# Hyena mixer, last MLP and grouped-query mixer of a diffusion trunk rebuilt, GpSimdE's element-wise work on VectorE

## The chip, the cores and the metric

One core of a Trainium2 chip runs the whole program in one launch. The metric is the device time of one execution in microseconds (us), the median of several runs. The engines are TensorE (PE; PEld is its weight load), VectorE (DVE), ScalarE (ACT), GpSimdE (POOL) and SyncE (SP), which issues the DMAs.

## What is computed

One step of a transformer-like trunk of four layers on 640 tokens (128 of context, 512 latent ones on a grid of 64 columns) of width 1024, all in float32. Each layer is a mixer and a squared-ReLU MLP of hidden width 4096, with modulation ahead of each and a gated, normalised residual after each. The mixers are differential attention, neighbourhood attention, grouped-query attention and a Hyena convolution. The parts that the change touches, shortened:

```python
def centred_short_conv(u, w, b):
    up = jnp.pad(u, ((0, 0), (1, 1), (0, 0)))
    return up[:, :L] * w[0] + up[:, 1:L + 1] * w[1] + up[:, 2:L + 2] * w[2] + b

def long_conv(z, freq_resp):
    zf = jnp.fft.rfft(z, n=2 * L, axis=1)
    return jnp.fft.irfft(zf * freq_resp[None], n=2 * L, axis=1)[:, :L]

def hyena(h, ...):
    parts = jnp.split(centred_short_conv(h @ w_in, short_w, short_b), 3, axis=-1)
    z = parts[0]
    for o in range(2):
        z = parts[o + 1] * (long_conv(z, freq_resp[:, o]) + z * filter_bias[o])
    return z @ w_o

# grouped-query attention: q and k are RMS-normalised per head, scaled, turned by the axial rotary
# every sublayer: x = layer_norm(ALPHA * x + gate * sublayer(modulate(x, shift, scale)), g, b)
# MLP: square(relu(h @ w1)) @ w2
```

## The kernel before

Every float32 product runs as three TensorE products of split operands: a high part and a low part of each side (`mm3`, lines 473 to 475). So each operand is split once: ScalarE rounds the high part and VectorE subtracts to get the low part (`w_convert` for weights, lines 450 and 451; `ln_out` for the activations `hh` and `hl`, lines 740 and 742; `k_stack` and similar helpers in the attention mixers). In `ln_out` the subtraction of the latent half for three of the five token tiles stands on GpSimdE.

A sublayer ends with its output product in quarters of 256 columns. `residual` multiplies each by the gate on VectorE (line 653) and adds it to the running sum `r` (line 660) on VectorE or GpSimdE, by a counter. Then the statistics of the norm are taken per token tile (line 689) and the next sublayer's input is formed. The norm's own scale and shift of `r` (`ln_tile`, lines 748 and 749, four 512-column steps per tile) follow behind.

The filters of the Hyena layer are made during earlier layers (`hy_filter` work, lines 1600 to 1624): a 512-column product, a window, a sum on VectorE and a difference on GpSimdE (line 1619, the "taps"), and a store to `ab_d`.

The third mixer projects both key pairs first, takes the reciprocal root of their mean squares, and, in `tail`, spreads that factor by TensorE (`rk`), turns the key with the rotary tables, whose swapped copy `sw` comes by DMAs from the other partitions, scales it, and stacks high and low parts of the key pair and of the cached key (`k_stack`). The query heads then follow in a stream of units, of which the first for context keys begins with the product `sc` (line 2203) of `qc`.

The Hyena mixer works in four groups of 256 channels and two orders, so eight times: the input is transposed and split (`zt`), multiplied by a DFT matrix in two halves of the frequencies (`kt`), and for each half VectorE forms sums and differences of the spectrum (line 1771), four 256-column products `pi` (line 1779; three of them on GpSimdE), one 1024-column product `pr` (1780), the combinations (1781 to 1784), ScalarE and VectorE split the result into `yy` (1785, 1788), and TensorE multiplies it back (`py`, 1798 and 1801). `feed` puts products of the next group's input projection (`hyin`) in between. One room, `hywork`, holds the intermediate values of both halves. The short convolution (`hy_conv`, line 1713) is a chain of fused steps on rows that are interleaved in pairs.

Within an MLP, chunks of four hidden tiles are closed by products with `w2` in quarters of 256 columns and collected in `sums` (line 882).

TensorE's order of work is mostly set by a tile scheduler from the order of the code; the waits follow from it.

## Time and profile before

| | |
|---|---|
| Time, median of 3 runs (lowest, highest) | 3380.49 us (3379.76, 3384.22) |
| Profiled execution | 3378.87 us, span 3376.8 us |
| Mean granted TensorE clock | 0.993 |
| Busy: TensorE, VectorE, ScalarE, GpSimdE | 97%, 71%, 46%, 11% |
| GpSimdE, us and instructions | 385.7 us, 476 |

The span is the time from the first to the last instruction in the trace; the execution's time adds what lies around it. A share of busy time is a mean over stages with different limits, so that 97% says how much TensorE could give back at most and not where. Starts in the rows below are in us from the beginning of the span.

### The profile page before, as it was taken

Reading aid. Unit: us, or ns where it says so; the run is one execution under the profiler, and the core shown is the slowest. Engines: PE = TensorE matmul, PEld = TensorE weight load, DVE = VectorE, ACT = ScalarE, POOL = GpSimd, SP = SyncE. Lnnn points to the kernel's source line nnn. Section 1 sums busy time; section 2 is a strip of 40 time slices with the busy share of each in tenths; the row PEclk is TensorE's granted clock in tenths of the full one; section 3 lists DMA queues with packets and bytes.
Section 4 is the critical chain, followed back from the end, with each engine's and each line's share of the span. In section 5 each row is a group of like instructions: output and inputs, shape, how many; then the busy total and the mean of one; then the engine's idle time right before and its main releaser. Section 6 shows DMA issues by size and latency. Waiting matters only on the chain.

```text
span 3376.8 us, 63034 instructions
## 1 busy us (share of the span) xinstructions
PE 3278.9 (97%) x25288; PEld 3162.6 (94%) x25288; DVE 2396.6 (71%) x4682; ACT 1552.0 (46%) x2832; POOL 385.7 (11%) x476
## 2 busy tenths in 40 slices
PE   8999999999999999999998999999999999999998
PEld 6888999998999899999997889999998999999998
DVE  4777877877765685777678878667769888723347
ACT  3667654333455654334345655433334334432322
POOL 0000101111322310000121020000021112100002
PEclk9999999999999999999999999999999999999999
DMA  8454245554343325556321123555523233222321
GB/s 287 143 158 129 65 149 177 174 189 150 102 139 101 120 83 187 169 188 214 118 72 48 36 66 105 173 177 181 185 68 127 84 114 134 96 76 76 101 76 51
DMA packets 162757, 429.40 MB, mean 127 GB/s; under 512 B 20574, under 2 KB 30438, under 8 KB 159390
## 3 DMA queue, kind: packets, MB, share of 16 engines
q1 hardware_dynamic: 162464, 425.37, 39.0%
q8 instruction: 199, 3.26, 0.4%
q14 instruction: 94, 0.77, 0.1%
HBM read 371.20 MB, written 34.05 MB: 120 GB/s over the span
## 4 chain that ended last, share of the span: by engine, by line
PE 78%; DVE 10%; issue 4%; ACT 3%; DMA 2%; POOL 2%; SPq 0%; DVEq 0%; POOLq 0%; ACTq 0%
PE w L473 18%; PE w L474 17%; PE w L475 17%; PE qk L473 3%; PE qk L474 2%; PE qk L475 2%; PE s L2038 2%; PE ptp L1088 2%; PE pv L2085 2%; PE pv L2189 1%; PE v L475 1%; PE py L1801 1%; PE v L474 1%; PE v L473 1%; DVE hl L451 1%
## 5 line engine op out<-in xcount | busy, mean ns | idle before, releaser
L451 DVE TENSOR_TENSOR hl<-raw,hl 128x1024 fp32r<-128x1024 f32 x411 | 515.9, 1256 | 395.4 <-ACT hl L450 378.2
L474 PE MATMUL w<-hl,ff 128*128 128x256 f32 x2560 | 714.2, 279 | 0.0
L475 PE MATMUL w<-hl,ff 128*128 128x256 f32 x2560 | 713.7, 279 | 0.0
L473 PE MATMUL w<-hl,ff 128*128 128x256 f32 x2560 | 713.6, 279 | 0.0
L450 ACT CAST hl<-raw 128x1024 fp32r<-128x1024 f32 x411 | 430.1, 1047 | 573.5 <-PE w L475 477.9
L473 PE MATMUL w<-hh,hl 128*128 128x320 f32 (+2 forms) x2048 | 637.0, 311 | 7.2 <-ACT fx L894 6.7
L474 PE MATMUL w<-hl,hl 128*128 128x320 f32 (+2 forms) x2048 | 633.3, 309 | 3.3 <-DVE hl L742 3.3
L475 PE MATMUL w<-hh,hl 128*128 128x320 f32 (+2 forms) x2048 | 633.2, 309 | 0.0
L474 PEld LDWEIGHTS w<-hl,ff 128*128 128x128 f32 x2560 | 480.7, 188 | 1.7
L473 PEld LDWEIGHTS w<-hl,ff 128*128 128x128 f32 x2560 | 480.4, 188 | 1.7
L475 PEld LDWEIGHTS w<-hl,ff 128*128 128x128 f32 x2560 | 479.6, 187 | 0.0
L541 DVE SCALAR_TENSOR_TENSOR ada<-adaw,sil,ada 128x512 f32<-128x512 f32 x504 | 358.0, 747 | 95.4 <-DMA adaw<-in_ada_w 92.6
L473 PEld LDWEIGHTS w<-hh,hl 128*128 128x128 f32 x2048 | 385.1, 188 | 23.1 <-ACT fx L894 9.5
L474 PEld LDWEIGHTS w<-hl,hl 128*128 128x128 f32 x2048 | 385.1, 188 | 4.1 <-DVE hl L742 4.1
L475 PEld LDWEIGHTS w<-hh,hl 128*128 128x128 f32 x2048 | 385.3, 188 | 0.0
L894 ACT ACTIVATE fx<-w 128x640 f32<-128x640 f32 (+2 forms) x136 | 91.5, 672 | 465.0 <-PE w L475 448.3
L882 DVE TENSOR_TENSOR sums<-sums,w 128x256 f32<-128x256 f32 x400 | 164.1, 415 | 128.4 <-PE w L475 127.9
L473 PE MATMUL qk<-hh,hl 128*128 128x320 f32 (+2 forms) x672 | 214.5, 319 | 0.2
L474 PE MATMUL qk<-hl,hl 128*128 128x320 f32 (+2 forms) x672 | 210.9, 314 | 1.7 <-DVE hl L742 1.7
L660 POOL TENSOR_TENSOR r<-r,gtmp 128x256 f32<-128x256 f32 x146 | 120.7, 834 | 782.6 <-DVE gtmp L653 739.6
L475 PE MATMUL qk<-hh,hl 128*128 128x320 f32 (+2 forms) x672 | 209.3, 311 | 0.0
L473 PE MATMUL w<-hl,oh 128*128 128x256 f32 x640 | 184.0, 288 | 7.6 <-DVE gtmp L653 5.4
(342 smaller groups left out, 6734.9 us busy)
## 6 DMA issues: line engine op xcount, KB each, us to landing
raw<-in_w SPq DMA_DIRECT2D x256, 512.0 KB
adaw<-in_ada_w SPq DMA_DIRECT2D x288, 256.0 KB
adaw<-in_ada_w SPq DMA_DIRECT2D x16, 1024.0 KB
raw<-ab_d SPq DMA_DIRECT2D x32, 512.0 KB
raw<-in_hy_in SPq DMA_DIRECT2D x24, 512.0 KB
ks<-ks SPq DMA_DIRECT2D x64, 160.0 KB
adaw<-in_ada_s SPq DMA_DIRECT2D x8, 1024.0 KB
raw<-in_da_qk SPq DMA_DIRECT2D x16, 512.0 KB
```

Source lines behind the costliest of these rows:

```text
L450: self.nc.scalar.copy(t[:, 0], raw)
L451: self.nc.vector.tensor_sub(t[:, 1], raw, t[:, 0].bitcast(F32))
L473: mm(ps, w[0], x[0], start=start, stop=False)
L474: mm(ps, w[0], x[1], start=False, stop=False)
L475: mm(ps, w[1], x[0], start=False, stop=stop)
L541: nc.vector.scalar_tensor_tensor(out=y, in0=raw[h], scalar=x, in1=y, op0=ALU.mult, op1=ALU.add)
L660: eng.tensor_add(rv, rv, tmp)
L882: nc.vector.tensor_add(v, v, ps)
L894: nc.scalar.activation(x, src, AF.Relu)
L1088: nc.tensor.transpose(ps[:, i * P:(i + 1) * P], pr[:, (done + i) * P:(done + i + 1) * P], self.ident)
L2038: mm(ps[dst], hd["qs"][h][:, self.qs], ks[:, c], start=n == 0, stop=n == 1)
L2085: nc.tensor.matmul(ps[64 * h:64 * h + 64], self.v[:, self.chunk + c, vc:vc + 64], pts[h][:, c * P:(c + 1) * P], start=c == 0, stop=c == se ...
```

## The change

- All residual adds, all subtractions of `ln_out`, the taps, the rotary products, and the low parts of `k_stack` in the third mixer are on VectorE. The scaling of the context units' output (line 2218, two mixers) goes from GpSimdE to two ScalarE steps. GpSimdE keeps the neighbourhood bias, the last norm and zeroing.
- Third mixer: of the norm of `r` left over from the MLP ahead, three of five tiles are taken during the keys' projection and two after the first key pair is stacked. One reciprocal root serves both key pairs; only the first pair is turned, scaled and stacked ahead of the query stream, the second in steps within it.
- Hyena: both halves' spectra are formed ahead of the first half's filtering, in rooms of their own; the `pi` products are two 512-column steps. The short convolution works on rows with eight columns of padding, on 512 columns at a time.
- Last MLP: chunks 0 to 5 are closed with products of 512 columns, 720 for 1440, with `w2` packed for it.

The core of the diff:

```diff
@@ residual
-        eng = nc.vector if quick or self.scale_r or self.rt < self.share else nc.gpsimd
...
-            eng.tensor_add(rv, rv, tmp)
+            nc.vector.tensor_add(rv, rv, tmp)
@@ ln_out
-            sub = nc.gpsimd.tensor_sub if h == 0 and t in (0, 2, 3) else nc.vector.tensor_sub
-            self.last_dve = sub(self.hl[:, f, c], x, self.hh[:, f, c].bitcast(F32))
+            self.last_dve = nc.vector.tensor_sub(self.hl[:, f, c], x, self.hh[:, f, c].bitcast(F32))
@@ mlp
+        def wide_close(ch):
+            for h in range(2):
+                pss = [self.any1([P, 512], "w2") for _ in range(NT - 1)]
+                if h == 0:
+                    two = self.b2([P, 2, 512], "w2")
+                pss.append(two[:, h])
+                for kp in range(2):
+                    u = self.wget(("w2", l, 4 * ch + 2 * h + kp))
+                    for t, ps in enumerate(pss):
+                        c = slice(t * P, (t + 1) * P)
+                        for k in range(2):
+                            f = slice(k * 512, (k + 1) * 512)
+                            self.mm3(ps, (ff[ch][:, 0, 2 * kp + k, c], ff[ch][:, 1, 2 * kp + k, c]), (u[:, 0, f], u[:, 1, f]), kp + k == 0, kp + k == 2)
+                        if kp:
+                            collect(ps, t, h * 512, ch == 0)
...
+            if last and ch < 7:
+                wide_close(ch - 1)
+                continue
@@ third mixer
             for i, x in enumerate(xk):
...
+                for t in ((NT - 1, 0), (1,))[i]:
+                    with self.tc.issue_after(self.last_dve.ins):
+                        self.ln_tile(t)
+            next(values)
+            next(values)
+            for i in range(2):
+                sums(sqs[i], list(factors(i))[1])
+            self.rsqrt(*factors(None), 1.0 / 64)
+            wides = [spread(0)]
+            turn_key(0, xk[0])
+            next(values)
+            next(values)
+            scale_key(0, xk[0], wides[0])
+            self.man.close()
+            for h in range(2):
+                stack_key(0, xk[0], h)
+            later = [lambda: turn_key(1, xk[1]), lambda: scale_key(1, xk[1], spread(1)), lambda: stack_key(1, xk[1], 0), lambda: stack_key(1, xk[1], 1)]
+            with self.tc.issue_after(self.stacked.ins):
+                for t in (2, 3):
+                    self.ln_tile(t)
@@ filter taps
-            nc.gpsimd.tensor_sub(v[:, 256:512], win[:, 0:256], win[:, 256:512])
+            nc.vector.tensor_sub(v[:, 256:512], win[:, 0:256], win[:, 256:512])
@@ hy_conv
-        acc(xl[:, 0, 1:], ul[:, 1, 0:n], w0)
-        acc(xl[:, 0, 0, 1:], ul[:, 1, n, 0:r], w0)
-        acc(xl[:, 1], ul[:, 0], w0)
-        acc(xl[:, 0], ul[:, 1], w2)
-        acc(xl[:, 1, 0:n], ul[:, 0, 1:], w2)
-        acc(xl[:, 1, n, 0:r], ul[:, 0, 0, 1:], w2)
+        acc(y, u[:, base - ROWS:end - ROWS], w0)
+        for e in range(2):
+            acc(xl[:, e], pairs(u[:, base + ROWS:end + ROWS])[:, e], w2, pairs(y)[:, e])
@@ hy_order
-            for q in range(2):
-                for s in range(2):
-                    eng = nc.vector if q * s else nc.gpsimd
-                    eng.tensor_mul(pi[:, q, s], z4[:, q, s], h4[:, q, 1 - s])
+        def filtered(kt):
+            z4, h4 = zs[kt], hs[:, kt]
+            for s in range(2):
+                nc.vector.tensor_mul(pi[:, :, s], z4[:, :, s], h4[:, :, 1 - s])
             nc.vector.tensor_mul(pr, z4, h4)
...
+        for kt in range(2):
+            spectrum(kt)
+        filtered(0)
+        feed(FB)
+        back(0)
+        filtered(1)
+        feed(FC)
+        back(1)
```

Three places show how the order moves. The first is VectorE in one Hyena order, from the products of the first half on (`hywork` the shared room, `hs` the filter's spectrum, `zf` the forward product). Before:

```order
L1771 TENSOR_TENSOR hywork<-zf_30730,hywork 128x512 x2
L1779 TENSOR_TENSOR hywork<-hywork,hs_30647 128x256
L1780 TENSOR_TENSOR hywork<-hywork,hs_30647 128x1024
L1782 TENSOR_TENSOR hywork<-hywork 128x2x256
L1781 TENSOR_TENSOR hywork<-hywork 128x2x256
L1784 TENSOR_TENSOR hywork<-hywork 128x512 x2
L1713 SCALAR_TENSOR_TENSOR x_30796<-u_30553,hsw,x_30796 128x127
L1788 TENSOR_TENSOR yy_30729<-hywork,yy_30729 128x512 x2
```

and now:

```order
L1846 TENSOR_TENSOR hywork<-zf_30752,hywork 128x512 x2
L1851 TENSOR_TENSOR hywork<-hywork,hs_30666 128x2x256 x2
L1852 TENSOR_TENSOR hywork<-hywork,hs_30666 128x1024
L1853 TENSOR_TENSOR hywork<-hywork 128x2x256
L1854 TENSOR_TENSOR hywork<-hywork 128x2x256
L1846 TENSOR_TENSOR hywork<-zf_30780,hywork 128x512 x2
L1856 TENSOR_TENSOR hywork<-hywork 128x512 x2
L1778 SCALAR_TENSOR_TENSOR x_30846<-u_30572,hsw,x_30846 128x127
L1778 SCALAR_TENSOR_TENSOR cv_30851<-u_30572,hsw,cv_30851 128x512
```

The four `pi` products, of which only one stood here (the other three are on GpSimdE), are two VectorE steps, and the second half's sums (line 1846 with another `zf`) stand ahead of the first half's output. The second place is VectorE at the third mixer's start, around the key's factors (`ss` the sums of squares, `r` the residual in its norm). Before, after eighteen of the norm's twenty steps:

```order
L749 TENSOR_TENSOR r_13383<-r_13383,ln_b_18377 128x512
L749 TENSOR_TENSOR r_13383<-r_13383,ln_b_18381 128x512
L1405 COPY misc_20120<-ss_20381 128x10
L1405 COPY misc_20120<-ss_20438 128x10
L1170 TENSOR_SCALAR misc_20120<-misc_20120 128x10
L451 TENSOR_TENSOR hl_20577<-raw_20134,hl_20577 128x1024
L1171 TENSOR_SCALAR misc_20120<-misc_20120 128x10
```

and now, after ten of the twelve that stand there:

```order
L752 TENSOR_TENSOR r_13390<-r_13390,ln_b_18385 128x512
L752 TENSOR_TENSOR r_13390<-r_13390,ln_b_18389 128x512
L457 TENSOR_TENSOR hl_20538<-raw_20142,hl_20538 128x1024
L1430 COPY misc_20128<-ss_20410 128x10
L1430 COPY misc_20128<-ss_20417 128x10
L1195 TENSOR_SCALAR misc_20128<-misc_20128 128x20
```

and behind the first key's stacking (`kk`), where the remaining eight begin:

```order
L1084 TENSOR_TENSOR kk<-x_20138,kk 64x512
L1086 TENSOR_TENSOR kk<-x_20138,kk 64x512
L1084 TENSOR_TENSOR kk<-x_20138,kk 64x512
L1086 TENSOR_TENSOR kk<-x_20138,kk 64x512
L751 TENSOR_TENSOR r_13390<-r_13390,ln_g_18383 128x512
L751 TENSOR_TENSOR r_13390<-r_13390,ln_g_18387 128x512
```

Eight of the norm's twenty steps moved from ahead of the factors to behind the first key, and one root works on twenty columns for two on ten. The third place is TensorE in the last MLP, within a closing product, where one token tile gives way to the next (`ff` the hidden values, `hl` here the split weights, `w` the sums in PSUM). Before, the end of one tile's twelve products and the start of the next:

```order
L473 MATMUL w_35841<-hl_35718,ff_35062 128x256
L474 MATMUL w_35841<-hl_35718,ff_35062 128x256
L475 MATMUL w_35841<-hl_35718,ff_35062 128x256
L473 MATMUL w_35855<-hl_35718,ff_35062 128x256
L474 MATMUL w_35855<-hl_35718,ff_35062 128x256
L475 MATMUL w_35855<-hl_35718,ff_35062 128x256
```

and now, the end of a tile's six from one weight unit and the start of the next tile's:

```order
L479 MATMUL w_34268<-hl_34150,ff_33721 128x512
L480 MATMUL w_34268<-hl_34150,ff_33721 128x512
L481 MATMUL w_34268<-hl_34150,ff_33721 128x512
L479 MATMUL w_34269<-hl_34150,ff_33721 128x512
L480 MATMUL w_34269<-hl_34150,ff_33721 128x512
L481 MATMUL w_34269<-hl_34150,ff_33721 128x512
```

Each product covers 512 columns in place of 256; a tile gets six in a row from one weight unit, and six more from the next unit after the other four tiles have had theirs.

## Rows read from the trace of the kernel before

**Rows 1.** The page, part 1: busy us, share of the span, instructions.
```profile
PE 3278.9 (97%) x25288; PEld 3162.6 (94%) x25288; DVE 2396.6 (71%) x4682; ACT 1552.0 (46%) x2832; POOL 385.7 (11%) x476
```

**Rows 2.** TensorE's waits: line, releaser, us in total, times, longest.
```profile
PE py L1801 <- ACT yy L1785: 12.2, 14, 1.2
...
PE w L473 <- ACT fx L894: 6.7, 5, 4.2
...
PE sc L2203 <- DVE qc L1475: 5.7, 1, 5.7
```

**Rows 3.** Windows: start:end, length, busy us of PE, PEld, DVE, ACT, POOL; clock; DMA.
```profile
2617.00:2654.00 37.00, 35.35 (x264) 35.10 (x264) 30.60 (x61) 14.27 (x24) 6.61 (x6) 1.00 0.28 97
...
2930.00:3360.00 430.00, 429.94 (x3303) 429.68 (x3302) 191.52 (x307) 131.04 (x177) 12.90 (x10) 1.00 0.24 77
...
1705.00:1740.00 35.00, 34.15 (x290) 33.70 (x290) 32.07 (x83) 25.71 (x50) 6.07 (x6) 1.00 0.26 82
...
1905.00:1965.00 60.00, 57.55 (x527) 51.11 (x526) 54.59 (x150) 41.15 (x96) 7.65 (x8) 1.00 0.14 42
...
1782.00:1789.00 7.00, 4.36 (x18) 4.39 (x19) 4.81 (x10) 4.19 (x5) 0.00 (x0) 0.51 0.02 4
```

**Rows 4.** Groups of GpSimdE's instructions, whole run: busy us, mean ns, idle before.
```profile
L660 POOL TENSOR_TENSOR r<-r,gtmp 128x256 f32<-128x256 f32 x146 | 120.7, 834 | 782.6 <-DVE gtmp L653 739.6 <-DVE m L2043 24.7 <-DVE mv L691 15.2
...
L1619 POOL TENSOR_TENSOR ab<-win 128x256 f32<-128x256 f32 x40 | 52.7, 1317 | 311.6 <-DVE win L1613 135.1 <-DVE win L1616 100.7 <-issue 37.4
...
L1779 POOL TENSOR_TENSOR hywork<-hywork,hs 128x256 f32<-128x256 f32 x48 | 52.3, 1116 | 228.0 <-DVE hywork L1771 228.0
...
L742 POOL TENSOR_TENSOR hl<-h,hh 128x512 fp32r<-128x512 f32 x21 | 30.3, 1442 | 102.8 <-ACT hh L740 102.8
```

**Rows 5.** Timeline of TensorE, first MLP: start, us, line, operation.
```profile
849.98 0.28 PE L475 MATMUL w<-hl,ff 128*128 128x256 f32 x1
850.10 0.40 PE L1609 MATMUL filt<-hl,hab 128*128 128x512 f32 x1
850.34 0.40 PE L1610 MATMUL filt<-hl,hab 128*128 128x512 f32 x1
850.57 0.28 PE L473 MATMUL w<-hl,ff 128*128 128x256 f32 x1
```

**Rows 6.** Timeline of VectorE in one Hyena order.
```profile
2641.18 1.22 DVE L451 TENSOR_TENSOR hl<-raw,hl 128x1024 fp32r<-128x1024 f32 x1
...
2647.96 1.29 DVE L1771 TENSOR_TENSOR hywork<-zf,hywork 128x512 f32<-128x512 f32 x2 [3.15 <-ACT hywork L1769]
...
2649.73 1.75 DVE L1780 TENSOR_TENSOR hywork<-hywork,hs 128x1024 f32<-128x1024 f32 x1
...
2652.11 0.69 DVE L1782 TENSOR_TENSOR hywork<-hywork 128x512 f32<-128x512 f32 x1 [0.63 <-POOL hywork L1779]
```

**Rows 7.** Timeline of VectorE at the third mixer's start.
```profile
1740.31 1.29 DVE L748 TENSOR_TENSOR r<-r,ln_g 128x512 f32<-128x512 f32 x2
1741.51 1.29 DVE L749 TENSOR_TENSOR r<-r,ln_b 128x512 f32<-128x512 f32 x2
...
1760.56 0.83 DVE L1422 TENSOR_TENSOR x<-x,tab 128x640 f32<-128x640 f32 x1 [3.36 <-DMA sw<-x]
...
1772.48 0.82 DVE L1423 TENSOR_TENSOR x<-x,sw 128x640 f32<-128x640 f32 x1 [3.75 <-POOL sw L1421]
```

**Rows 8.** Timeline of SyncE's queue there.
```profile
1755.43 2.45 SPq L1030 DMA_DIRECT2D sw<-x  x4
```

**Rows 9.** Timeline of GpSimdE and ScalarE, first MLP.
```profile
749.56 1.93 POOL L1619 TENSOR_TENSOR ab<-win 128x256 f32<-128x256 f32 x1 [1.13 <-DVE win L1616]
...
764.98 0.63 ACT L795 ACTIVATE ln_b<-ln_b 128x512 f32<-128x512 f32 x1 [0.81 <-DMA ln_b<-in_ln_b]
```

**Rows 10.** Groups of VectorE's instructions from 1705 to 1740 us.
```profile
L689 DVE BATCH_NORM_STATS2 st<-r 128x6 f32<-128x512 f32 x10 | 6.9, 690 | 2.2 <-POOL r L660 2.0
...
L451 DVE TENSOR_TENSOR hl<-raw,hl 128x1024 fp32r<-128x1024 f32 x3 | 4.7, 1556 | 0.0
```

More of the change, by code (lines that the diff above doesn't have):

```diff
@@ L40 @@
 F1N = 2
-QM = 1
-QL = 4
-QW = 1
 AHD = 1
@@ L197, in unit_b, with unit_w, close_units @@
     return w[k0 * P:(k0 + 4) * P, c0:c0 + 256].reshape(4, P, 256).transpose(1, 0, 2).reshape(P, 1024)
+def unit_w(w, k0, c0):
+    return w[k0 * P:(k0 + 2) * P, c0:c0 + 512].reshape(2, P, 512).transpose(1, 0, 2).reshape(P, 1024)
+def close_units(w, ch, wide):
+    if wide and ch < 6:
+        return [unit_w(w, 4 * ch + 2 * kp, h * 512) for h in range(2) for kp in range(2)]
+    return [unit_b(w, 4 * ch, q * 256) for q in range(4)]
 def prepare(inp):
@@ L870, in mlp @@
         nc = self.nc
-        self.share = QL if last else QM
         ff = {}
@@ L1438, in mixer_gq @@
             for i in (1, 0):
-                t = [self.S(F32, f"tab{i}{s}") for s in range(2)]
+                t = [self.scratch(TOK, f"tab{i}{s}", 1) for s in range(2)]
                 for s in range(2):
@@ L1442, in mixer_gq, with feed @@
                 tab[i] = t
+            self.man.enter_context(self.tc.manual_schedule(engines={mybir.EngineType.PE}))
+            sqs = []
             for i, x in enumerate(xk):
-                sq = self.S(F32, "sq")
                 for _ in ks[i]:
                     pass
+                sq = self.S(F32, "sq")
                 nc.scalar.activation(sq, x, AF.Square)
-                late.append((i, x, sq))
-            for x in late:
-                tail(*x)
+                sqs.append(sq)
+                for t in ((NT - 1, 0), (1,))[i]:
[12 more added lines that the diff above has]
+            self.man.close()
+            for h in range(2):
+                stack_key(0, xk[0], h)
[3 more added lines that the diff above has]
+                    self.ln_tile(t)
+            def feed(j, n):
+                fd.feed(j, n)
+                if later and j:
+                    later.pop(0)()
             heads = {}
@@ L1670, in hy_in_gen @@
         for gr, p in parts:
-            us = [self.S(F32, "u") for _ in range(2)]
+            us = [self.scratch(TOK + 2 * ROWS, "u", 4) for _ in range(2)]
             opening = bool(self.pending)
@@ L1685, in hy_in_gen @@
                     if part == 0:
-                        nc.scalar.copy(us[ct][:, c0:c1], ps)
+                        self.hy_put(us[ct], ps, c0, c1)
                         continue
@@ L1696, in hy_in_gen @@
                 if split == 256:
-                    nc.scalar.copy(us[ct][:, c0:c1], ps)
+                    self.hy_put(us[ct], ps, c0, c1)
                 elif part:
-                    nc.scalar.copy(us[ct].rearrange("p (a b) -> p a b", a=2), pss[ct][:, :, :HALF])
+                    for i in range(2):
+                        self.hy_put(us[ct], pss[ct][:, i, :HALF], i * HALF, i * HALF + HALF)
                 if part == 0:
@@ L1706, in hy_in_gen, with hy_put @@
             self.settle()
+    def hy_put(self, u, ps, c0, c1):
+        for a, b, off in ((0, CTX, 0), (CTX, TOK, ROWS)):
+            lo, hi = max(a, c0), min(b, c1)
+            if lo < hi:
+                self.nc.scalar.copy(u[:, lo + off:hi + off], ps[:, lo - c0:hi - c0])
     def hy_conv(self, x, u, w):
@@ L2217, in scores @@
             nc.vector.reciprocal(m[:, 4:6], m[:, 2:4])
-            nc.gpsimd.tensor_mul(e, e, m[:, 4:6].unsqueeze(2).to_broadcast([P, 2, P]))
+            for h in range(2):
+                nc.scalar.mul(e[:, h], e[:, h], m[:, 4 + h:5 + h])
             yield
```

94 lines of the change are left out of this document (49 added, 45 removed).

## The prediction

> **What bounds the kernel now.** I read the page's line of busy times first [rows 1]: TensorE is busy for 3278.9 of 3376.8 us, so all that any change to the other engines can give back is some part of the 98 us in which it is idle, plus what a lowered clock costs. The list of its waits comes next [rows 2], because it says where those 98 us lie. Three entries touch this change: 14 waits of the Hyena order's inverse transform (`py`) for ScalarE's `yy`, 12.2 us together; one wait of 5.7 us for `qc` where the third mixer's query stream starts; 4.2 us (the longest of five) for `fx` in the first MLP. Then windows [rows 3], to see what the other engines have left in each place. In one Hyena order (37 us) VectorE is busy for 30.6 us and GpSimdE for 6.6; in the last MLP TensorE is busy 429.94 of 430.00 us and VectorE 191.5; in the last 35 us ahead of the third mixer VectorE is busy for 32.1; within its stream, 54.6 of 60. So the Hyena waits are waits for a chain, not for a full engine; the last MLP has no idle time to win; and the two other places have little VectorE time to spare. The profiled execution took 3378.87 us, 2.07 beyond its span and 1.62 under the median of 3380.49: I make the sum on the trace and set it on the median.
>
> **Hyena orders.** Before, three of each half's four 256-column imaginary products stand on GpSimdE at 1116 ns [rows 4]. They start with the spectra, take 3.3 us in a row, and VectorE waits 0.63 us for the last [rows 6]; its own 1024-column product takes 1.75 us beside them, where a split of the same width takes 1.22 with GpSimdE idle [rows 6]. After, VectorE does all. Its 512-column step costs 0.65 us (half of 1.29 for two [rows 6]), its 1024-column step 1.2. From the end of the first forward product to the first `py`: ScalarE's copy 0.65 (taken like a VectorE step of this width), two sums 1.3, two imaginary products 1.3, the real one 1.2, two combinations 1.3, the second spectrum's two sums 1.3 (they stand in between now), the first output 0.65, its rounding on ScalarE 0.65: 8.35 us. TensorE has meanwhile, in the new order, 15 input products, the second forward product (24 of 256 columns), then 33 more input products. At 0.1175 us per 256 columns [rows 5], and 0.147 for 320 by proportion, that is 7.06 + 2.82 = 9.9 us. The first wait goes, with 1.5 us to spare. The second half: VectorE goes on with the second output 0.65, the low parts 1.3, convolution taps some 2.1, two weight splits 2.4, and the second half's products, combinations and first output 4.45, and ScalarE rounds: 19.25 us from the same start; TensorE gets there after 9.9 + 2.8 + 48 x 0.147 = 19.75. The second wait goes too, but only just: in one of the two orders two more steps (1.0 us) stand ahead of it. I take 11 of the 12.2 us; bounds 0 (both chains late by what they are late today) and 12.2. The convolution's taps become fewer (2.4 for 3.0 us, counting columns), which VectorE has time for either way.
>
> At this place the Trainium skill, "SBUF — State Buffer", section "Who interferes with whom", bears on the row: a VectorE instruction with two SBUF inputs contends with a GpSimdE instruction that reads SBUF, and whichever holds the shared port makes the other wait for a whole instruction. The 1.75 against 1.22 us goes that way; by the rule alone the product could be held by 1.1 us, not 0.53, so I keep the row.
>
> **Third mixer's start.** Before, VectorE puts twenty 512-column steps of the residual's norm ahead of the keys' factors, 12.1 us from 1740.3 at 0.605 each [rows 7] (a pair starts 1.2 us after the one ahead). SyncE is held behind weight loads that need VectorE's splits, so the swapped keys' copies are issued at 1755.4 [rows 8], VectorE starts on the first key at 1760.6 after 3.4 us of waiting for them, and on the second only at 1772.5 after 3.75 us for GpSimdE's product [rows 7]. Both keys and then the query come before the `sc` wait of 5.7 us. In the new order twelve norm steps (three tiles) stand there, eight follow the first key's stacking, and the second key goes into the stream. Worked forward: norm 7.3 us to 1747.6 and two splits 2.4 to about 1750, so the copies are issued about 5 us earlier and land near 1755.5; first key's turn, 2.5 us; scaling 1.0; eight low parts, some 3.5; to about 1763; eight norm steps 4.8, to 1768; the query's copy and its rotary products 2.5, near 1775 with its own copies' landing. TensorE, with the same filler ahead of `sc`, comes there at 1784.6 - 5.7 = 1779. The wait goes with some 4 us to spare. In the 7 us around it the granted clock was 0.51 [rows 3], that is the 1.2 GHz level, after a stall of 5.7; its 4.36 busy us would have been 2.2 us shorter. Gain 7.9. Against it: in the stream VectorE takes the eight rotary products at 0.82 (its own of that size [rows 7]), the second key, about 7, and the residual adds, some 6: 20 us in a stretch of about 225 that runs at 91% [rows 3]. What GpSimdE no longer holds up returns a part. I charge 1 us: net gain 7, bounds -3 (the stream loses 3, and the wait half remains) and 8.
>
> **First MLP.** ScalarE stands on `ln_b` until 764.98 [rows 9], then does the `fx` for which TensorE has waited 4.2 us. That load was issued on SyncE's queue behind the store of `ab`, which waited for the tap on GpSimdE, 1.93 us there [rows 9]; on VectorE a 256-column step is 0.33 (half of 0.65). If the rest of the queue moves with it, the load comes 1.6 us earlier. I take 2 us with the clock that a shorter stall keeps; bounds 0 (another load is the late one) and 5.
>
> **Sublayer ends.** There are eight. Of GpSimdE's 146 residual adds and 21 subtractions [rows 4], three of each lie in the last 35 us before such an end. On VectorE: 3 x 0.33 + 3 x 0.65 = 2.9 us more, where it has 35 - 32.1 = 2.9 left [rows 3]. But 2.0 of its idle time there was spent waiting for GpSimdE's `r`, and its three splits take 1.56 us instead of 1.22 [rows 10, 6], 1.0 in all. The two nearly cancel: 0, bounds -4 and +8 over the eight. The rest of the 146 adds, and the 40 taps elsewhere, lie under TensorE work where VectorE has idle time, as in the last MLP (45% busy [rows 3]): 0.
>
> **Last MLP.** 1440 products of 256 columns become 720 of 512. The starts in [rows 5] are 0.12 us after a 256-column product, 0.24 and 0.23 after 512-column ones: time goes by columns, 720 x (0.235 - 2 x 0.1175) = 0. Rounding of the starts allows 0.003 us per product: bounds -2 and +2. VectorE collects in half as many steps of double width, with half its time free. The Trainium skill, "TensorE: Matmul & The Clock Gate", section "Wait — 56ns, not 53.3ns?", gives each matmul a fixed part of about 2.5 ns beyond its columns. By it this edit would save an estimated 720 x 0.0025 = 1.8 us, and the sum would be 1.8 us lower; the rows here show no fixed part, so I leave it out.
>
> **Sum.** -11 - 7 - 2 + 0 + 0 = -20 us: 3380.5 - 20 = 3360.5 us.
>
> **Rivals.** (1) The second Hyena wait stays, because VectorE now carries the whole chain: 81 to 84% of an order, and half a microsecond to spare by my count. Against it speaks that VectorE loses the wait for GpSimdE and the stretched steps. Then about 5 of the 11 us come: 3367. (2) The chains were late for another reason, ScalarE's or SyncE's, and the change moves nothing that TensorE sees: the waits of [rows 2] reappear under new names, 3377. The rows that name GpSimdE as releaser speak against it. (3) The other side: VectorE becomes the last engine at the sublayer ends. The 2.9 us more per end come without the relief and each end stalls by them; stalls there grow towards the length after which the clock was at 0.51 [rows 3], and a 7 us stretch of that costs 2.2. Eight times 2.9 + 2.2 is 41 us, less the 20 gained: 3401. It decides from 2.5 + 0.9 = 3.4 us per end, where 27 us are lost and the time is over 3387. For it: 32.1 of 35 us busy. Against: the wait for `r` in [rows 10]. (4) More than I count: GpSimdE's part of 386 us no longer stretches VectorE anywhere, so further short waits go, and both bounds of the third mixer and the first MLP come in: 3348.
>
> **Chances.** Forecast 0.48, (1) 0.22, (2) 0.12, (3) 0.06, (4) 0.12. The range of 3342 to 3376 takes in (1) and (4) and the bounds of the terms, and leaves out (3) and most of (2). A change under 0.2%, 6.8 us, could not be told from none here; below 3373.7 counts as faster: forecast, (1), (4), together 0.82; within, 0.12; slower 0.06.
>
> **What would show it.** Right: the `py` entry of TensorE's waits nearly empty and an order near 35.5 us; no wait at `sc` beyond 1 us and no lowered clock there; the last MLP still 430 us; GpSimdE near 100 us busy. Wrong: waits at `hl` or `w` at the sublayer ends over 1.5 us, `py` waits released by VectorE, `s` or `ptp` waits in the third mixer's stream adding up to more than 4 us.

## The result and the profile after

| | before | after |
|---|---|---|
| Median (lowest, highest), 4 runs each | 3380.32 us (3379.76, 3384.22) | 3342.67 us (3341.09, 3343.22) |
| Profiled execution, span | 3378.87, 3376.8 us | 3342.79, 3340.9 us |
| Mean granted TensorE clock | 0.993 | 0.995 |

The ratio is 0.9888 [0.9872, 0.9903]: 37.7 us faster, where 20 were forecast. The time lies 0.7 us inside the lower edge of the range of 3342 to 3376.

Where the time went shows best by stage. The table gives the distance from a stage's first TensorE product to the next stage's, read from the timelines of both profiles; "output" is the mixer's output product. Between runs in which a stage's code is the same, such a distance varies by up to 3.6 us in differential attention (391.5 to 395.1), 2.9 in the neighbourhood's output (80.2 to 83.1) and 2.4 in the first MLP (488.3 to 490.7), and by less elsewhere.

| Stage, us | before | after | difference | forecast |
|---|---|---|---|---|
| Differential attention, with output | 392.2 | 393.1 | +0.9 | 0 |
| First MLP | 494.7 | 490.7 | -4.0 | -2 |
| Neighbourhood attention | 240.8 | 240.3 | -0.6 | 0 |
| its output | 82.3 | 80.2 | -2.1 | 0 |
| Second MLP | 495.7 | 495.4 | -0.3 | 0 |
| Third mixer | 210.6 | 206.1 | -4.5 | -7 |
| its output | 109.7 | 108.7 | -1.1 | 0 |
| Third MLP | 488.1 | 488.1 | +0.1 | 0 |
| Hyena, to its output's start | 293.8 | 279.7 | -14.1 | -11 |
| its output (the last order's end lies in it) | 80.6 | 75.1 | -5.5 | 0 |
| Last MLP | 454.6 | 448.8 | -5.8 | 0 |

The page's busy times after, to be held against [rows 1]:

```profile
PE 3265.2 (98%) x24568; PEld 3122.5 (93%) x24568; DVE 2424.6 (73%) x4790; ACT 1559.5 (47%) x2922; POOL 97.0 (3%) x235
```

GpSimdE fell by 289 us and VectorE rose by 28; TensorE's own busy time fell by 13.7, which isn't a wait over 0.2 us: it lies in the products themselves and in their clock. Of TensorE's waits after (line, releaser, us in total, times, longest), these matter:

```profile
PE ptp L1113 <- ACT e L2295: 3.2, 1, 3.2
PE s L2121 <- ACT e L2195: 3.1, 3, 2.2
...
PE hyin L479 <- DVE hywork L1846: 2.4, 3, 0.8
PE w L479 <- ACT fx L898: 2.3, 4, 0.6
PE w L479 <- ACT hh L744: 2.1, 4, 0.5
...
PE w L480 <- DVE hl L745: 1.4, 4, 0.3
```

Against [rows 2], `py` for `yy` and `sc` are gone, and of 6.7 us for `fx` 2.3 are left, none over 0.6. New are 2.4 us at `hyin`, where Hyena's `hywork` is late, the waits at `hh` where there had been `hl` alone, and 3.2 us at `ptp` in the third mixer's stream (those for `e` at `s` came to 3.1 us before, too, the longest 2.0). The windows that answer to [rows 3], in the same order without the stream's middle, and with one of its start added:

```profile
2603.00:2640.00 37.00, 36.91 (x280) 36.61 (x280) 31.21 (x58) 14.72 (x34) 0.40 (x6) 1.00 0.28 97
2895.00:3325.00 430.00, 429.42 (x2615) 399.22 (x2614) 191.43 (x267) 132.49 (x171) 13.78 (x11) 1.00 0.23 76
1700.00:1735.00 35.00, 33.92 (x285) 33.26 (x284) 32.78 (x86) 25.59 (x51) 0.00 (x0) 1.00 0.22 73
1771.00:1778.00 7.00, 6.98 (x49) 6.75 (x48) 6.84 (x18) 5.68 (x7) 0.00 (x0) 1.00 0.24 77
1804.00:1814.20 10.20, 4.92 (x21) 4.20 (x22) 7.91 (x24) 5.14 (x17) 0.00 (x0) 0.50 0.16 52
```

An order of Hyena keeps TensorE busy 36.91 of 37 us, and VectorE 31.2. In the last MLP, busy throughout as before, there are 2615 records for 3303. Ahead of the third mixer VectorE has 2.2 us left of 35. From `sc` on, which now starts at 1771.3, the clock is 1.00, where it was 0.51. The last row is the price: 10.2 us near the stream's start with TensorE busy for 4.9 at a clock of 0.50, that is at 1.2 GHz.

### The profile page after: what moved, and what is told of

Its sections match the earlier page's. It is cut to its first block, busy times and chain, and to the rows that moved or that the text cites. A ratio compares the mean times of both kernels' runs of the same rounds, so it can differ in the third digit from the quotient of the medians.

```text
span 3340.9 us, 61106 instructions
## 1 busy us (share of the span) xinstructions
PE 3265.2 (98%) x24568; PEld 3122.5 (93%) x24568; DVE 2424.6 (73%) x4790; ACT 1559.5 (47%) x2922; POOL 97.0 (3%) x235
## 3 DMA queue, kind: packets, MB, share of 16 engines
q1 hardware_dynamic: 162464, 425.37, 38.5%
## 4 chain that ended last, share of the span: by engine, by line
PE 88%; DVE 6%; ACT 3%; DMA 2%; issue 1%; SPq 0%; DVEq 0%; ACTq 0%
PE w L479 19%; PE w L480 19%; PE w L481 19%; PE qk L479 3%; PE qk L480 3%; PE qk L481 3%; PE s L2121 3%; PE ptp L1113 2%; PE pv L2168 2%; PE hyin L479 1%; PE hyin L480 1%; PE hyin L481 1%; PE pv L2272 1%; PE v L481 1%; PE v L479 1%; PE v L480 1%
## 5 line engine op out<-in xcount | busy, mean ns | idle before, releaser
L457 DVE TENSOR_TENSOR hl<-raw,hl 128x1024 fp32r<-128x1024 f32 x411 | 502.6, 1224 | 450.4 <-ACT hl L456 449.3
L481 PE MATMUL w<-hl,ff 128*128 128x256 f32 (+1 forms) x2320 | 674.0, 291 | 0.0
L480 PE MATMUL w<-hl,ff 128*128 128x256 f32 (+1 forms) x2320 | 673.6, 290 | 0.0
L479 PE MATMUL w<-hl,ff 128*128 128x256 f32 (+1 forms) x2320 | 672.9, 290 | 0.0
L480 PEld LDWEIGHTS w<-hl,ff 128*128 128x128 f32 x2320 | 435.7, 188 | 11.9
L479 PEld LDWEIGHTS w<-hl,ff 128*128 128x128 f32 x2320 | 435.2, 188 | 11.4
L481 PEld LDWEIGHTS w<-hl,ff 128*128 128x128 f32 x2320 | 434.9, 187 | 9.3
L547 DVE SCALAR_TENSOR_TENSOR ada<-adaw,sil,ada 128x512 f32<-128x512 f32 x504 | 357.2, 747 | 82.3 <-DMA adaw<-in_ada_w 78.7
L886 DVE TENSOR_TENSOR sums<-sums,w 128x256 f32<-128x256 f32 (+1 forms) x350 | 156.1, 454 | 69.2 <-PE w L481 68.6
L479 PE MATMUL w<-hl,oh 128*128 128x256 f32 x640 | 183.3, 287 | 2.2 <-DVE gtmp L659 0.8
L481 PE MATMUL w<-hl,oh 128*128 128x256 f32 x640 | 180.4, 283 | 1.0 <-DVE oh L1099 0.9
```

Source lines behind the costliest of these rows:

```text
L457: self.nc.vector.tensor_sub(t[:, 1], raw, t[:, 0].bitcast(F32))
L479: mm(ps, w[0], x[0], start=start, stop=False)
L480: mm(ps, w[0], x[1], start=False, stop=False)
L481: mm(ps, w[1], x[0], start=False, stop=stop)
L547: nc.vector.scalar_tensor_tensor(out=y, in0=raw[h], scalar=x, in1=y, op0=ALU.mult, op1=ALU.add)
L886: nc.vector.tensor_add(v, v, ps)
```

## The experiments

Each is an edit of the changed kernel, but for the second, which edits the kernel before. Differences are against the kernel before on the same chip (the changed kernel: -37.7). Its median differed by up to 3 us between chips.

**Products on GpSimdE again.** The theory: `py` waited for GpSimdE's products. The rival: for TensorE's order or the convolution.

```diff
-            for s in range(2):
-                nc.vector.tensor_mul(pi[:, :, s], z4[:, :, s], h4[:, :, 1 - s])
+            for q in range(2):
+                for s in range(2):
+                    eng = nc.vector if q * s else nc.gpsimd
+                    eng.tensor_mul(pi[:, q, s], z4[:, q, s], h4[:, q, 1 - s])
```

> The changed kernel with three of four imaginary products of each half on GpSimdE again, 256 columns each, in the new order with both spectra first. Theory (GpSimdE's three products in a row are what the inverse transform waited for; the new order alone gives 1.5 us of cover to the first half and 0.5 to the second): the chain is 1.5 us longer per half, the first wait stays away, the second comes back at about 1 us, seven times: 3350, from 3347 to 3354. Rival (the new order alone removed the waits): 3342 to 3345.

Measured: 3350.88 us, -28.5, so 9 slower than with them on VectorE. TensorE's waits in Hyena (columns as above):

```profile
PE py L1877 <- ACT yy L1860: 6.8, 7, 1.1
PE py L1877 <- DVE gtmp L659: 1.7, 2, 1.5
```

Seven waits for `yy` are back, about 1 us each, as the theory had it, with nothing else touched; the Hyena output's multiply in front of `py` holds TensorE for 1.7 us, where it was 1.3. The theory holds. It doesn't explain all of the 9: in Hyena up to its output TensorE is idle for 11.6 of 288.9 us here and 6.5 of 279.7 after, and the other 4.1 us lie in time that the trace shows as busy.

**The products alone, in the kernel before.** The reverse of that edit, in the kernel before (`pi` in two VectorE steps of 512 columns).

> The kernel before with the imaginary products as two 512-column steps on VectorE, nothing else changed. Theory (GpSimdE's products are the chain's late part): VectorE's chain is shorter by the 0.63 us wait and the 0.53 of the stretched product and longer by 0.8, and GpSimdE's last product no longer ends it; each of the 14 waits is shorter by some 0.4 us, 3380.3 - 6 = 3374. Rival (the order, one spectrum after the other with too little work between, is the cause): the waits stay within 0.2 us each, 3378 to 3381.

Measured: 3364.22 us, -15.1, where I had expected -6. All 14 `py` waits over 0.2 us are gone, not only shorter, and Hyena takes 281.3 us to its output, 12.5 less: the 12.2 of [rows 2]. One wait of before stands there still, the 4.1 us at `zf` for `zt`. VectorE's first steps of one half, start and duration in us:

```profile
2645.25 1.29 DVE L1777 TENSOR_TENSOR hywork<-hywork,hs 128x512 f32<-128x512 f32 x2
2646.47 1.22 DVE L1778 TENSOR_TENSOR hywork<-hywork,hs 128x1024 f32<-128x1024 f32 x1
```

The 1024-column product takes 1.22 us, where it took 1.75 beside GpSimdE's in [rows 6]. By the Trainium skill, "SBUF — State Buffer", section "Who interferes with whom", this is the shared port, and the trace agrees. GpSimdE's second and third product in the kernel before, around VectorE's of 2649.73 to 2651.48:

```profile
2649.48 0.92 POOL L1779 TENSOR_TENSOR hywork<-hywork,hs 128x256 f32<-128x256 f32 x1
...
2650.37 1.72 POOL L1779 TENSOR_TENSOR hywork<-hywork,hs 128x256 f32<-128x256 f32 x1
```

GpSimdE's product in flight ends 0.67 us into VectorE's, which loses 0.53; the next starts while VectorE is at work, ends 0.61 us behind it, and takes 1.72 us for 0.92. So each engine seems to have waited for the other's instruction, VectorE only for the rest of one already begun. The 1.1 us that the prediction took from this rule are the most, for an instruction just begun; the row doesn't speak against the rule.

**Old order of the halves.** Spectrum, filter and inverse of the first half, then of the second, with everything else of the change.

```diff
         for kt in range(2):
             spectrum(kt)
-        filtered(0)
-        feed(FB)
-        back(0)
-        filtered(1)
-        feed(FC)
-        back(1)
+            filtered(kt)
+            feed(FB if kt == 0 else FC)
+            back(kt)
```

> The changed kernel with each half's spectrum, filter and inverse transform one after the other again, products all on VectorE, convolution in its new form. What is open: the kernel before waited 4.1 us for zt in the first order with a lowered clock, and still did with the products on VectorE (x4); the changed kernel and x3 do not. Theory 1 (spectra first leaves TensorE other work ahead of the late half): the wait comes back at 3 to 4 us, and the orders lose 0.2 us each: 3342.7 + 6 = 3349. Theory 2 (the convolution's fewer steps let VectorE reach zt in time): no wait over 1 us there, 3342 to 3345. Either way the waits of py stay under 0.3 us each, as in x4.

Measured: 3341.06 us, -38.2. No `py` wait, and hardly one at `zf`:

```profile
PE hyin L479 <- ACT h L740: 2.7, 2, 1.4
...
PE zf L480 <- DVE zt L1099: 0.2, 1, 0.2
```

The new order isn't needed for these waits: it moves work that was in time anyway. It even brought one: the 2.4 us at `hyin` for `hywork` are gone here, and Hyena takes 278.3 us to its output, 1.4 less than after. The wait of 4.1 us at `zf` is gone here too, as it is in the run above with the products on GpSimdE, and in those below with adds or subtractions there; only the kernel before's convolution has it. So it went with the new convolution. This is by elimination, as the convolution was not put back by itself.

**Residual adds on GpSimdE again**, three of four, as before (in `mlp` and the outputs a share of them stays on VectorE).

```diff
+        self.rt = (self.rt + 1) % 4
+        eng = nc.vector if quick or self.scale_r or self.rt < self.share else nc.gpsimd
...
-            nc.vector.tensor_add(rv, rv, tmp)
+            eng.tensor_add(rv, rv, tmp)
```

> The changed kernel with the residual adds shared between GpSimdE and VectorE again by the old counter, all else as changed. Theory (a GpSimdE add of 834 ns holds the three buffers of the gated product, so the output products wait): the Hyena output stretch, which fell by 5.5 us, grows back by 4 to 6, the neighbourhood output by 2, the grouped-query output by 1, the other ends by 0 to 1 each; in all 3352, from 3349 to 3355. Rival (these stretches gained because VectorE and GpSimdE no longer meet elsewhere): no stretch moves by more than 1 us, 3342 to 3346.

Measured: 3339.26 us, -40.1. Half of the theory holds: Hyena's output takes 77.3 us, 2.2 more than after and more than in any other run of the changed kernel. The neighbourhood's takes 82.85, 2.6 more, and the third mixer's 0.8 more, but the run with the second key later, in which that code is untouched, had 82.7 and 0.9 more, too. And at the sublayer ends no wait for `hh` or `hl` is left, against 4.7 us after (the rows above and 1.2 in mixers), and the time ends no higher. VectorE's adds help under Hyena's output product and hurt at the ends.

**Adds on GpSimdE only at the ends.** The same lines, with the share set per place: all on VectorE but for three of four in the last quarter of each sublayer.

```diff
+        self.share = QE
         u = unit(0, 4)
...
+        self.share = 4
         self.w_convert(self.wi + 4)
```

> The changed kernel with the residual adds on VectorE as changed, but within a sublayer's end (the last quarters and the norm's statistics) three of four of those that may wait on GpSimdE, by the old counter. Theory after the first runs (adds on GpSimdE cost 5.6 us in three mixers' output stretches, where they follow each other closely, and save about 1 us at each sublayer end, where VectorE is full): output stretches as in the changed kernel within 1 us, no wait for hh or hl at the boundaries (1.0 to 1.3 us each now), 3342.7 - 6 = 3337, from 3334 to 3340. Rival (what the first run gained at the boundaries came from adds far ahead of them): boundary waits stay, 3342 to 3344.

Measured: 3334.67 us (3332.52 to 3336.14), -42.8 and some 5 better than the change, though the intervals of the two ratios still touch. The waits for `hh` and `hl` are gone, and the outputs are as short as after.

**Subtractions on GpSimdE again**, three of five token tiles' latent half in `ln_out`.

```diff
-            self.last_dve = nc.vector.tensor_sub(self.hl[:, f, c], x, self.hh[:, f, c].bitcast(F32))
+            sub = nc.gpsimd.tensor_sub if h == 0 and t in (0, 2, 3) else nc.vector.tensor_sub
+            self.last_dve = sub(self.hl[:, f, c], x, self.hh[:, f, c].bitcast(F32))
```

> The changed kernel with three of seven low-part subtractions of each sublayer end on GpSimdE again (1.3 to 1.4 us each there, 0.65 on VectorE), adds on VectorE. Theory (at the ends VectorE's queue of small steps is what is late, and the subtraction is on the path itself, so that GpSimdE's longer one takes back what the relief gives): waits of 0.8 to 1.1 us for hl per boundary as in the kernel before, 3341 to 3345. Rival 1 (any relief of VectorE does, as the adds did): no waits there, 3335 to 3338. Open besides: the first MLP was 494.7 us before and 487 to 491 in all runs of the changed kernel, with the taps on either engine; if it is 494 here, the subtractions are the cause.

Measured: 3340.53 us, -39.7. The waits at the ends move to the norm's transposes (`lnt`):

```profile
PE lnt L734 <- ACT r L704: 6.5, 6, 1.4
...
PE lnt L734 <- DVE r L706: 1.8, 4, 0.4
```

8.3 us wait there in place of the 4.7 at `hh` and `hl`, and the time is no longer for it. Neither theory nor rival holds: where the subtraction stands decides which wait is seen, and the sum of waits over 0.2 us doesn't tell the time.

**Narrow close.** The last MLP's chunks closed in quarters of 256 columns, with `w2` packed as before.

```diff
-            if last and ch < 7:
+            if False and last and ch < 7:
```

> The changed kernel with the last MLP closed in 256-column products again, w2 packed as before. Theory (each product has a part that does not go by columns, 5.1 ns by the two paces of the trace): each of six closes 27.5 to 28.3 us, 3342.7 + 3.7 = 3346.4. Rival 1 (a part of 2.5 ns each): 3344.5. Rival 2 (the faster pace of the two last chunks, 54.4 us for 56.4, also comes with the width): 3348.5, and those chunks are back at 56.4. Rival 3 (no part of it is the width): 3342.7.

Measured: 3345.24 us, -34.1; the last MLP takes 455.5 us, 6.75 more than after. The first and the last start of one whole close, in TensorE's timeline, after (512 columns) and here (256):

```profile
3048.61 0.39 PE L479 MATMUL w<-hl,ff 128*128 128x512 f32 x1
...
3075.84 0.39 PE L481 MATMUL w<-hl,ff 128*128 128x512 f32 x1
```

```profile
3048.63 0.28 PE L479 MATMUL w<-hl,ff 128*128 128x256 f32 x1
...
3076.78 0.28 PE L481 MATMUL w<-hl,ff 128*128 128x256 f32 x1
```

And the first and the last of the 480 products of 256 columns that end the program, which are the same code in both kernels, after and here:

```profile
3271.11 0.28 PE L479 MATMUL w<-hl,ff 128*128 128x256 f32 x1
...
3325.53 0.28 PE L481 MATMUL w<-hl,ff 128*128 128x256 f32 x1
```

```profile
3274.34 0.28 PE L479 MATMUL w<-hl,ff 128*128 128x256 f32 x1
...
3330.76 0.28 PE L481 MATMUL w<-hl,ff 128*128 128x256 f32 x1
```

A close of 120 products of 512 columns has 119 steps in 27.23 us, 228.8 ns each; one of 240 of 256 columns has 239 in 28.15, 117.8 each, twice which is 235.6. That is 0.80 us less per close. The closing 480 products take 54.42 us after (113.6 ns) and 56.42 here (117.8). Six times 0.80 and 2.0 is 6.8 of the 6.75 us. By stage this is the second rival; the median shows less of it (3.6 us more than the change), as the first MLP, which the edit doesn't touch, is 2.4 shorter in this run. In the kernel before the first close ran at 113.3 ns and was as short as a wide one within 0.3, the other five and the closing 480 at 117.8: 5 x 0.80 - 0.3 + 2.0 = 5.7 of the 5.8 us.

**Wide close in every MLP**, with `w2` packed for it and the filters' steps taken within the close.

```diff
-            if last and ch < 7:
+            if ch < 7:
```

> The changed kernel with the first six chunks of all four MLPs closed in 512-column products, w2 packed alike. Theory (0.8 us per close, where the pace of 256 columns was 117.8 ns, none where it was 113.3): about 12 of 18 closes gain, 3342.7 - 10 = 3333, from 3331 to 3336. Rival 1 (a fixed part of 2.5 ns per product): -5.4, 3337. Rival 2 (filter products, which take the same PSUM buffers in the first three MLPs, now wait for the open tile): 3341 to 3346.

Measured: 3339.21 us, -38.3. Second and third MLP are 4.8 and 4.6 us shorter than after. The first is 4.0 longer, and the neighbourhood's output, which the edit doesn't touch, 2.9 longer, of which 1.7 is a stretch at a clock of 0.51. Of the two MLPs' gains, 1.8 us each come in the closing products, at 113.3 ns for 117.8. Why the first loses is not shown.

**Taps on GpSimdE again** (line 1619 of before).

```diff
-            nc.vector.tensor_sub(v[:, 256:512], win[:, 0:256], win[:, 256:512])
+            nc.gpsimd.tensor_sub(v[:, 256:512], win[:, 0:256], win[:, 256:512])
```

> The changed kernel with the filter taps' difference on GpSimdE again, nothing else. Theory (the tap on GpSimdE delays a store on SyncE's queue, behind it a norm's scale and shift, and so ScalarE): the wait of 4.2 us for fx in the first MLP comes back with a lowered clock, that MLP takes 494 us for 488 to 491, 3342.7 + 5 = 3348. Rival 1 (that stall hangs on another load's time): no wait over 1 us, 3341 to 3344. Rival 2 (GpSimdE's taps lengthen VectorE's work): several small waits, at most 2 us more.

Measured: 3341.19 us, -36.3, first MLP 489.3. The 4.2 us wait for `fx` doesn't come back; its total is 3.9 us and the longest 1.6. ScalarE's queue, after and then here:

```profile
762.49 0.63 ACT L801 ACTIVATE ln_b<-ln_b 128x512 f32<-128x512 f32 x1
763.03 0.68 ACT L898 ACTIVATE fx<-w 128x640 f32<-128x640 f32 x1
763.93 0.63 ACT L801 ACTIVATE ln_g<-ln_g 128x512 f32<-128x512 f32 x1 [0.22 <-DMA ln_g<-in_ln_g]
```

```profile
761.70 0.63 ACT L801 ACTIVATE ln_g<-ln_g 128x512 f32<-128x512 f32 x1 [0.64 <-DMA ln_g<-in_ln_g]
762.40 0.63 ACT L801 ACTIVATE ln_b<-ln_b 128x512 f32<-128x512 f32 x1
762.94 0.69 ACT L898 ACTIVATE fx<-w 128x640 f32<-128x640 f32 x1
```

After, `fx` stands between two pairs of loaded tiles that ScalarE scales (`ln_g`, `ln_b`); with the taps back it stands behind both pairs, as before. SyncE issues the loads no earlier after (758.95 us) than before (755.70), so my step, an earlier store and so an earlier load, didn't happen.

**Second key later** in the third mixer's stream.

```diff
-                if later and j:
+                if later and j > 1 and n % 2:
```

> The changed kernel with the second key pair's four steps at every other unit of the third and fourth head pair of the stream, not the first four units of the second. Theory (its turning and low parts, 4.0 us on VectorE, stand ahead of the softmax factors when the stream is short of work, and TensorE waits 2.2, 3.2 and 2.2 us): these three waits shrink to under 1.5 us each and the clock of 0.70 there stays up, 3342.7 - 5 = 3338, from 3335 to 3340. Rival (the stream's start waits for ScalarE's two scaling steps per context unit, or is as short of work without the key, as it was before): waits of 1.2 to 2 us stay there, 3341 to 3344.

Measured: 3341.71 us, -35.8; the third mixer takes 205.1 us to its output, 1.0 less, within what that stage varies. After, the stream's start shows in TensorE's and VectorE's timelines:

```profile
1806.11 0.90 PE L1113 MATMUL ptp<-ident,e 128*128 128x128 f32 x3 [2.21 <-DVE pt L1119]
1810.18 0.69 PE L1113 MATMUL ptp<-ident,e 128*128 128x128 f32 x2 [3.17 <-ACT e L2295]
...
1820.84 1.57 PE L2121 MATMUL s<-kk,qroom 128*128 128x320 f32 x5 [2.24 <-ACT e L2195]
```

```profile
1804.01 0.82 DVE L1438 TENSOR_TENSOR x<-x,tab 128x640 f32<-128x640 f32 x1
...
1807.97 0.16 DVE L2193 TENSOR_TENSOR m<-m,rs 128x1 f32<-128x1 f32 x1
```

The second key's turning (line 1438) stands ahead of the softmax factor (line 2193) on VectorE, as the theory had it. But with the key later TensorE waits just so:

```profile
1805.46 1.97 PE L2121 MATMUL s<-kk,qroom 128*128 128x320 f32 x6 [3.48 <-ACT e L2195]
```

And ScalarE's `e`, for which it waits, waits for VectorE:

```profile
1804.43 0.88 ACT L2195 ACTIVATE e<-s,m,rs 128x640 f32<-128x640 f32 x1 [3.33 <-DVE m L2193]
```

The rival's forecast holds, but for neither of its reasons. Where TensorE waits VectorE is busy for 12.6 of 13 us after (1798 to 1811) and for 8.8 of 9 here (1797 to 1806): it is full at the stream's start, and what it does first only sets where TensorE waits.

**The whole norm first**, five tiles ahead of the keys' factors.

```diff
-                for t in ((NT - 1, 0), (1,))[i]:
+                for t in ((NT - 1, 0), (1, 2, 3))[i]:
...
-            with self.tc.issue_after(self.stacked.ins):
-                for t in (2, 3):
-                    self.ln_tile(t)
```

> The changed kernel with all five tiles of the left-over norm ahead of the key factors, as in the kernel before, in place of three there and two behind the first key. Theory (the split of the norm is what makes the query ready in time; in the changed trace qc is ready as TensorE comes to it, with no time to spare): eight steps, 4.8 us, come back on the path to sc, which waits 3 to 5 us, with a lowered clock: 3342.7 + 5 = 3348, from 3345 to 3350. Rival (the second key's leaving was enough, with the 4 us of slack that I had counted): sc waits under 1 us, 3341 to 3344.

Measured: 3341.76 us, -38.5. No `sc` wait, and a clock of 1.00 from `sc` on (1769.8). Eight norm steps, 4.8 us, weren't what made `qc` late. That the second key left was enough for it is by elimination: it wasn't put back, and neither was GpSimdE's share of the mixer.

**Ends and wide closes together.** The share per place as above, and wide closes in all MLPs but the first (`if l and ch < 7`).

> A version meant to beat both: the changed kernel with the adds of the sublayer ends on GpSimdE again (as in x5), and 512-column closes in the last three MLPs (as in x8; the first MLP, which grew by 4 us there, keeps 256). If the two gains add, 5 us from the first and 4.7 us in each of the second and third MLP: 3342.7 - 14 = 3328, from 3325 to 3332. If GpSimdE's adds and the open PSUM tiles get in each other's way, one of them is lost: 3333 to 3338.

Measured: 3328.15 us (3326.78 to 3331.24), ratio 0.9848 [0.9833, 0.9863], -52.1. It beats both kernels, and in the median the gains add up: 5.1 of the adds and 9.4 of two MLPs are 14.5 of the 14.4 us beyond the change. That they agree so closely is in part luck: second and third MLP are 10.0 shorter than after, but the first is 4.0 longer than with the adds alone, and differential attention 5.0 shorter.

## Why the prediction was right in sign and short in size

The three terms that were forecast at 20 us gave 22.6. The other 14.4 us by stage, 11.3 of them in Hyena's output and the last MLP, came from stages that I had put at 0. That the time still lies in the range, by 0.7 us, is luck.

**Hyena's orders, -11 for -14.1: right, with one wait missed.** The `py` waits were GpSimdE's, as both runs on the products show. Against the forecast 11, 12.2 went and 2.4 came at `hyin`. Beside them stood a row of before that I passed over, in the list of waits and in the window behind it:

```profile
PE zf L474 <- DVE zt L1074: 4.1, 1, 4.1
```

```profile
2567.00:2570.50 3.50, 3.50 (x18) 3.50 (x18) 3.28 (x8) 2.07 (x5) 0.00 (x0) 0.51 0.51 179
```

A wait of 4.1 us, then 3.5 us at a clock of 0.51 (1.7 us lost). "Which VectorE has time for either way" failed: at Hyena's start it hadn't, and with the shorter convolution it is in time. All waits of this stretch add up to 17.9 us before and 6.2 after; 11.7 and 1.7 of clock make 13.4 of the 14.1. My count of the two halves' chains gave the new order a credit for timeliness that isn't its own, and missed the 2.4 us that it cost at `hyin`.

**Hyena's output, 0 for -5.5: wrong.** The step "the rest of the 146 adds ... lie under TensorE work where VectorE has idle time" failed, as the last order and the output share VectorE. The waits in this stretch, before, after, with the old order of halves, and in the kernel before with the products on VectorE:

```profile
PE w L473 <- DVE gtmp L653: 4.8, 3, 2.9
```

```profile
PE py L1875 <- DVE gtmp L659: 1.3, 1, 1.3
...
PE w L479 <- DVE gtmp L659: 0.2, 1, 0.2
```

```profile
PE w L479 <- DVE gtmp L659: 2.4, 1, 2.4
```

```profile
PE w L473 <- DVE gtmp L653: 3.3, 2, 2.9
```

`w` waits for a PSUM tile that VectorE must multiply by the gate (`gtmp`). VectorE's timeline before, ahead of the longest wait, which ends at 2856.5:

```profile
2851.89 1.78 DVE L1780 TENSOR_TENSOR hywork<-hywork,hs 128x1024 f32<-128x1024 f32 x1
2854.28 1.20 DVE L1782 TENSOR_TENSOR hywork<-hywork 128x512 f32<-128x512 f32 x1 [0.62 <-POOL hywork L1779]
2855.40 0.68 DVE L1781 TENSOR_TENSOR hywork<-hywork 128x512 f32<-128x512 f32 x1
2856.00 0.41 DVE L653 TENSOR_TENSOR gtmp<-w,gate 128x256 f32<-128x256 f32 x1
```

The multiply stands last behind a stretched product, a wait for GpSimdE and a sum. With the products on VectorE alone 1.5 of the 4.8 us go and the 2.9 stay, so for that wait the multiply's place in the queue counts, not the stretching. The new order of halves moves it: 2.4 us wait in the old order, 0.2 after, but then 1.3 at `py`, and the stretch is 75.5 us in the old order and 75.1 after, so little comes of it. In time, adds on VectorE are worth 2.2 us here and the products on VectorE 1.6 (79.0 for 80.6 in the kernel before). The remaining 1.7 of the 5.5 are what a lowered clock behind the wait of 2.9 us cost, before and, in the second row, with the products on VectorE:

```profile
2857.20:2860.60 3.40, 3.40 (x18) 3.40 (x18) 3.40 (x5) 1.14 (x2) 0.41 (x1) 0.50 0.22 19
```

```profile
2841.90:2845.30 3.40, 3.40 (x19) 3.40 (x18) 3.38 (x4) 0.66 (x2) 1.69 (x2) 0.50 0.00 0
```

In the changed kernel the clock is 1.00 in all of this stretch, and so it is with the adds on GpSimdE and with the old order of the halves; which edit keeps it up isn't isolated. Of the neighbourhood's 2.1 I claim only that it agrees with the 2.6 that adds on GpSimdE cost there, as two runs with that code untouched differed by 2.5 and 2.9, 1.7 of each at a lowered clock.

**Last MLP, 0 for -5.8: wrong.** "Time goes by columns" came from [rows 5], where a pair of 512-column products stands among others and has 0.235; the steady pace is 0.229. The Trainium skill's rule, "TensorE: Matmul & The Clock Gate", section "Wait — 56ns, not 53.3ns?", which I left out, points the right way, with 2.5 ns where 6.7 per wide product were measured. Neither is the whole: the same 256-column code runs at 113.6 ns in one kernel and 117.8 in the other. What chooses between these is open; no run here isolates it. The failed step is the price per product, and of the 5.8 us 2.0 came in the closing products, which the edit doesn't touch.

**Third mixer, -7 for -4.5: right, its charge too small.** The `sc` wait and its clock went as forecast, 5.7 and 2.1 us. Relative to the mixer's start, `qc` came 2 us later than by my count and TensorE 2 earlier, so that of the 4 us to spare 0.1 were left (1771.2 and 1771.3). The mixer to its output, before and after, and then the rest of the stream's time at the lowered clock, before and after (the first part of after is above):

```profile
1724.70:1935.30 210.60, 194.82 (x1579) 177.01 (x1577) 180.73 (x478) 127.67 (x284) 30.98 (x26) 0.98 0.18 50
...
1816.10:1819.50 3.40, 2.83 (x21) 2.43 (x22) 3.17 (x8) 1.43 (x3) 0.00 (x0) 0.50 0.36 135
```

```profile
1719.00:1925.10 206.10, 193.22 (x1579) 177.74 (x1577) 178.16 (x486) 130.95 (x297) 0.00 (x0) 0.97 0.18 54
...
1821.00:1824.40 3.40, 3.40 (x15) 3.33 (x16) 2.57 (x6) 1.97 (x6) 0.00 (x0) 0.50 0.13 31
```

TensorE's idle time fell from 15.8 to 12.9 us, 2.9 where 5.7 went at `sc`: the stream took back 2.8. The lowered clock there cost 4.2 us (half of 4.9 and 3.4) where it had cost 1.4, another 2.7. So the charge was 5.5 where I set 1: I had spread VectorE's 20 us over the whole stream, and at its start VectorE has no room. Of the 7.8 us that `sc` and its clock gave 2.3 are left. The other 2.2 of the 4.5 lie in the time of the products themselves, which no run isolates and my sum didn't have. The sign that I had set for being wrong, `s` and `ptp` waits of more than 4 us together in the stream, did come, with 10.4; but before they were 6.6, so that it was a poor sign.

**First MLP, -2 for -4.0: sign right, step wrong.** The wait list lost 4.4 us at `fx`, by ScalarE's order and landing times, not by the store. The clock behind that wait had been 0.50 from 764.8 to 771.6 us, with TensorE busy for 5.3, and is 1.00 after, which is 2.7 us more. That the stage gained only 4.0 of these 7.1 is partly this run's: in five runs with this MLP's code untouched it took 488.3 to 488.8 us, 6 less than before. Neither adds, taps nor subtractions put back bring it, so which edit moved ScalarE's queue is open.

**Sublayer ends, 0 for about -1: right.** 5.8 us at `hl` before (3.3 at the MLPs' starts, the rest at the mixers') against 4.7 at `hh` and `hl`: the two effects do nearly cancel. The two runs on adds show the one half, as with adds on GpSimdE and the subtractions on VectorE those waits are gone. Rival (3) had no part; the time is nearest rival (4), but its gains came from places other than those it names.

## What to carry to other kernels

Read the list of waits to its end before giving a stage 0: the 4.1 and 4.8 us lay in it. Move work by place, not by kind: here the same add saves time on VectorE under Hyena's output product and costs time at a sublayer's end, where the free engine does better, though it takes 0.83 us for 0.44. Take a matmul's price from a long steady stretch of its own, not from two starts.

## What was not expected of the hardware

A steady stream of 256-column products has two paces, 113.3 to 113.6 and 117.8 ns each, that stay through a whole segment; both of the closing ones lie in windows with a granted clock of 1.00. In every trace here the closing products of the last three MLPs run at 113.3 to 113.8 where the closes ahead of them are wide and at 117.8 where they are narrow: in the second and third MLP 117.8 after, and 113.3 with wide closes in every MLP. Those of the first MLP stay at 117.8 either way. Why is open. 512-column products took 228.8 to 229.1 ns in every long stretch. A VectorE step can keep TensorE waiting longer by standing behind others than by being slow: `gtmp` takes 0.41 us and TensorE waited 2.9 for it.
